# A gated-DeltaNet encoder layer: the products of k with k and q taken as split float32r products, half a batch at a time

## The chip, the cores and the metric

The kernel runs on one core of a Trainium2 chip. The metric is the device time of one execution in microseconds. An execution is one launch of the whole program: one encoder layer and the final norm, for a prompt of 1024 tokens and a sample of 256 tokens.

## The reference, cut to what matters

Each layer has a token-mixing block, a cross-attention into 256 memory tokens and a feed-forward block, for 1024 channels. The change lies in the token-mixing block's gated delta rule, which runs over 4 heads of 128 channels, forward and backward in time:

```
q = l2norm(heads(q, DN_DK)); k = l2norm(heads(k, DN_DK))
...
lower = where(strict, einsum('bhncd,bhnsd->bhncs', kb, k) * decay, 0.0)
tinv = triangular_solve(lower + eye, eye, ...)
u = einsum('bhncs,bhnsd->bhncd', tinv, v * beta[..., None])
a_intra = einsum('bhncd,bhnsd->bhncs', q, k) * decay
...
v_new = u_i - einsum('bhcd,bhde->bhce', w_i, state)
o = einsum('bhcd,bhde->bhce', qg_i, state) + einsum('bhcs,bhse->bhce', a_i, v_new)
state = state * exp(gl_i)[..., None, None] + einsum('bhcd,bhce->bhde', kg_i, v_new)
```

So every chunk of tokens needs two Gram matrices: the products of k with k, from which the triangular inverse comes, and the products of k with q, which weigh the chunk's own values.

## The kernel before, in words

**Numbers.** The large projections are float32 products split into float32r parts: an operand x becomes hi (x rounded by ScalarE's copy) and lo (x - hi), and a product is the sum of hi·hi, hi·lo and lo·hi (`mm3`, L110). The recurrence works with chunks of 128 tokens and with plain float32 products.

**Batches.** The 1280 tokens of 4 heads make 40 blocks of 128 x 128: each head's 1024 prompt tokens are one batch of 8 blocks (batches 0 to 3), the sample's 256 tokens of all four heads are the last (batch 4). `dn_batch` (L768) works through one batch: decays (L778 to L801), the products of k with k (L804 to L806), the inverse norms of k from their diagonals (L808 to L819, `rsqrt` at L230), the products of k with q and the matrices aT and X (L820 to L833), then X through DRAM into a layout in which VectorE solves 32 x 32 triangles (L837 to L865), back through DRAM into U and UT (L914 to L943), two levels of products that join the triangles (L946 to L984, whose first reads UT and X, "UT,gb" in the trace), and the scan over the blocks with its state (L988 to L1054).

**Names.** `dec` is the pair of decay tiles, one for each direction, in the tiles "gb0" and "gb1"; X is written over them in place (L832), so the trace says "gb". The tile `acc` is the convolved q, k or v, that is `q2`, `k2` and `v2`. `cw` holds the batch's columns of 8 numbers: ssk (the squared norms), r, r2, iv and bp.

**Order of work.** The program is written by a main generator (projections, tile by tile) and by side generators such as `dn_batch`. `mm` (L100) adds an estimate of each product to a clock; after each step of the main generator `pump` (L71) lets every side run whose time has come, and a side's `yield n` puts it off by n of that clock's nanoseconds. DEC is 1200. TensorE issues in the order in which this writes the program (L186). The order on the other engines is chosen at build time by the framework's scheduler, from when operands are ready in its own model of time. A matmul at the head of TensorE's queue that waits for somebody holds up all behind it, the main projections too.

**Banks.** PSUM is two pools of four banks of 512 float32 (L183, L184): `pm`, which the main projections use (one for each block of 512 or 256 tokens, until it is evacuated), and `pq` for small work. The products of k with k take two banks of `pm` for a batch, `pg` (L804); they hold them until X is made. The products of k with q take one bank of `pq` for each half (L823).

**Around it.** While the recurrence of one head runs, the main generator projects the next head's q, k and v (with their convolution, L696 to L752) and the gates (`gate_tile`), in plan order. The batches' scans overlap with the next batch's start: the decays and products of batch i + 1 are written when the inverse of batch i is done (`wait_for`, L776), beside batch i's scan. The tiles "UT0" and "UT1" (one buffer each) hold U's transposes until the inverse's end and the triangles (`XL`, L837) in between.

Of the kernel before, what the change touches and what calls it, by code (L numbers as in the profile page):

```python
# [9 lines left out]
F32R = mybir.dt.float32r  # L10
I32 = mybir.dt.int32
AF = mybir.ActivationFunctionType
ALU = mybir.AluOpType
# [4 lines left out]
P = 128  # L18
# [8 lines left out]
EPS = 1e-6  # L27
# [14 lines left out]
def f32(ap):  # L42
    return ap.bitcast(F32)


def quad(ps):
    return ps.rearrange("p (c t) -> p c t", t=P)
# [7 lines left out]
class Trunk:  # L55
# [44 lines left out]
    def mm(self, out, l, r, start=True, stop=True, more=False):  # L100
        n = 1
        for x in out.shape[1:]:
            n *= x
        if l.dtype == F32R:
            self.clock += max(n, 16) / 2.4 * (1 if n >= 256 else 4)
        else:
            self.clock += (4 * n / 2.4) if n > 1 else 2
        self.nc.tensor.matmul(out, l, r, start=start, stop=stop, skip_group_check=more)  # L108
# [59 lines left out]
def trunk_kernel(ctx: ExitStack, tc: tile.TileContext, a):  # L168
    nc = tc.nc
    V, S, G, T, SY = nc.vector, nc.scalar, nc.gpsimd, nc.tensor, nc.sync  # L170
    K = Trunk(ctx, tc, a)
    mm, mm3, tr, split = K.mm, K.mm3, K.tr, K.split
# [10 lines left out]
    pm = ctx.enter_context(pool("pm", 4, space=PSUM))  # L183
# [21 lines left out]
    two = lambda x: x.rearrange("h p (k n) -> p k h n", n=256)  # L205
# [11 lines left out]
    ident = cst[:, C_ID : C_ID + P]  # L217
# [6 lines left out]
    def bank(p=pq, tag="b"):  # L224
        return p.tile([P, 512], F32, tag=tag, name="bank")
# [4 lines left out]
    def rsqrt(y, x, scratch):  # L230
        V.tensor_scalar(out=y.bitcast(I32), in0=x.bitcast(I32), scalar1=-0.5, scalar2=float(0x5F3759DF), op0=ALU.mult, op1=ALU.add)
        for _ in range(3):
            V.scalar_tensor_tensor(out=scratch, in0=y, scalar=-0.5, in1=x, op0=ALU.mult, op1=ALU.mult)
            V.tensor_tensor(out=scratch, in0=scratch, in1=y, op=ALU.mult)
            end = V.scalar_tensor_tensor(out=y, in0=scratch, scalar=1.5, in1=y, op0=ALU.add, op1=ALU.mult).ins
        return end
# [176 lines left out]
    parts = []  # L413
# [9 lines left out]
    parts = [t[:, i * NS : (i + 1) * NS] for t in parts for i in range(2)]  # L423
# [3 lines left out]
    r = xp.tile([P, 512], F32, tag="nacc", name="seed", bufs=2)[:, :NS]  # L427
# [6 lines left out]
    hi, lo = x_h[2]  # L434
    rooms = [bank() for _ in range(3)]
    los = []
    for k in range(KT):
        if k in (5, 7):
            t = xp.tile([P, 512], F32, tag="nsq", name="nt", bufs=3)[:, :NS]
        else:  # L440
            at = min(k, 5)
            t = rooms[at % 3][:, at // 3 * NS : at // 3 * NS + NS]
# [3 lines left out]
        while los and (k == KT - 1 or los[0][0] < k):  # L446
            n, t = los.pop(0)
# [6 lines left out]
    pair = [(bank(), slice(512 * i, 512 * i + 512)) for i in range(2)]  # L454
# [32 lines left out]
    beta = cp.tile([P, 2, 40], F32, name="beta")  # L487
# [18 lines left out]
    s0, s1, var, rs, scr, mu = (sums[:, i, :] for i in range(6))  # L506
# [178 lines left out]
    qp = des.enter_context(pool("dn"))  # L685
# [73 lines left out]
    def big(tag, bufs=1):  # L759
        return qp.tile([P, 8, P], F32, tag=tag, name=tag, bufs=bufs)  # L760
# [3 lines left out]
    def wait_for(what, bi):  # L764
        while bi >= 0 and (what, bi) not in flags:
            yield 300

    def dn_batch(bi, qkv, chains):  # L768
        cs = slice(8 * bi, 8 * bi + 8)
# [3 lines left out]
        q2, k2 = qkv[:2]  # L773
        yield FIRST

        yield from wait_for("inverse", bi - 1)  # L776
        dec, bp, bpe, egl, eg, neg_eg = [], [], [], [], [], []
        for d in range(2):  # L778
            gb = big(f"gb{d}")
            SY.dma_start(gb, grd[d, cs, :].unsqueeze(0).to_broadcast([P, 8, P]))  # L780
            dec.append(gb)
        yield 2500
        for d in range(2):
            gb = dec[d]
# [16 lines left out]
            bp.append(bp_), bpe.append(bpe_), egl.append(egl_), eg.append(eg_), neg_eg.append(ne_)  # L801

        ssk, ssq, r, scr, r2, iv = (cw[:, i] for i in (0, 1, 2, 3, 6, 7))
        pg = [bank(pm), bank(pm)]  # L804
        for b in range(8):
            mm(pg[b // 4][:, (b % 4) * P : (b % 4 + 1) * P], k2[:, b, :], k2[:, b, :])  # L806
        junk = gs()[:, :P]
        for b in range(8):  # L808
            V.scalar_tensor_tensor(
                out=junk, in0=pg[b // 4][:, (b % 4) * P : (b % 4 + 1) * P], scalar=1.0, in1=ident, op0=ALU.mult, op1=ALU.mult,  # L810
                accum_out=ssk[:, b : b + 1])
            if b % 4 == 3:
                yield DEC
        V.tensor_scalar(out=scr, in0=ssk, scalar1=4.0 * EPS, scalar2=None, op0=ALU.add)
        rsqrt(r, scr, r2)
        V.tensor_tensor(out=r2, in0=r, in1=r, op=ALU.mult)
        V.scalar_tensor_tensor(out=iv, in0=r, scalar=0.5, in1=scr, op0=ALU.mult, op1=ALU.mult)
        for d in range(2):
            V.tensor_tensor(out=bp[d], in0=beta[:, d, cs], in1=r2, op=ALU.mult)  # L819
        aT = [big(f"aT{d}", 2) for d in range(2)]  # L820
        for hf in range(2):
            hs = slice(4 * hf, 4 * hf + 4)
            pa = bank()  # L823
            for c in range(4):
                mm(pa[:, c * P : (c + 1) * P], k2[:, 4 * hf + c, :], q2[:, 4 * hf + c, :])
            for d in range(2):
                V.tensor_tensor(out=aT[d][:, hs, :], in0=quad(pa), in1=dec[d][:, hs, :], op=ALU.mult)  # L827
            yield DEC
            for d in range(2):
                for c in range(4):  # L830
                    b = 4 * hf + c
                    V.scalar_tensor_tensor(out=dec[d][:, b, :], in0=pg[hf][:, c * P : (c + 1) * P], scalar=bp[d][:, b : b + 1], in1=dec[d][:, b, :], op0=ALU.mult, op1=ALU.mult)  # L832
                yield DEC  # L833
        X = dec

# [19 lines left out]
        for i in range(30, -1, -1):  # L855
            n, c = 32 - i, (i + 1) // 2
# [3 lines left out]
                out=t3, in0=u3[:, c:, i:],  # L860
                in1=XL[:, 32 * i + i : 32 * i + 32].unsqueeze(1).to_broadcast([P, m, n]), op=ALU.mult)
# [18 lines left out]
        for hf in range(2):  # L880
            hs = slice(4 * hf, 4 * hf + 4)
# [46 lines left out]
        for s in (0, 2):  # L928
            c = slice(16 * s, 16 * s + 16)
            SY.dma_start(own(UTm, s), vsd[bi][1, 0][:, c].rearrange("b c h j -> (c h) b j"))  # L930
            SY.dma_start(own(Um, s), vsd[bi][0, 1][:, c].rearrange("b c h j -> (c h) b j"))
        for s in range(4):
            c = slice(16 * s, 16 * s + 16)
# [14 lines left out]
        for level, mask in enumerate((m64, m128)):  # L948
# [7 lines left out]
            for hf, hs in enumerate(halves):  # L956
# [3 lines left out]
                for d in range(2):  # L960
                    V.scalar_tensor_tensor(
                        out=U[d][:, hs, :], in0=quad(pu), scalar=mine[:, 2 * level + d : 2 * level + d + 1], in1=U[d][:, hs, :],
                        op0=ALU.mult, op1=ALU.add)
# [34 lines left out]
        for step in range(nsteps):  # L998
            last = step == nsteps - 1
            for grp in groups:  # L1000
                ws, kg = {}, {}
                if not last:
                    for ch, (d, blks) in grp:
                        b = blks[step]
                        kg[ch] = sq128("sw", 6)
                        S.activation(kg[ch], ktm[:, b, :], AF.Copy, scale=bpe[d][:, b : b + 1])
                if step:
# [3 lines left out]
                    for i, (ch, (d, blks)) in enumerate(grp):  # L1011
                        b = blks[step]
# [4 lines left out]
                for i, (ch, (d, blks)) in enumerate(grp):  # L1017
                    b = blks[step]
                    mm(pc4(py, i), U[d][:, b, :], ws[ch] if step else vw[:, b, :])
                vt = {}  # L1020
                for i, (ch, (d, blks)) in enumerate(grp):
                    b = blks[step]
# [7 lines left out]
                if not last:  # L1030
# [3 lines left out]
                    for i, (ch, (d, blks)) in enumerate(grp):  # L1034
                        b = blks[step]
# [9 lines left out]
                for i, (ch, (d, blks)) in enumerate(grp):  # L1045
                    b = blks[step]
# [11 lines left out]
        for b in range(8):  # L1058
            junk = sq128("vt", 4)
# [398 lines left out]
    class OutProj:  # L1458
# [7 lines left out]
        def parts(self, m, b, ks, ps=None):  # L1466
            ps = bank(pm)[:, : BLOCKS[b][1]] if ps is None else ps
            if m == len(self.ws):
                self.ws.append(K.take())
            yield from proj(ps, self.ws[m], self.src, b, ks)  # L1470
            if (m, b) == (0, 0):
                K.ahead()
            self.first.append(ps)
# [224 lines left out]
    for h in range(HEADS):  # L1698
# [26 lines left out]
        if h == HEADS - 1:  # L1725
# [12 lines left out]
            for b in range(3):  # L1738
                hi, lo = o_h[b]
# [5 lines left out]
    op = OutProj(o_h, h3)  # L1745
# [116 lines left out]
    b12, r2 = ((Two(), Two()) for _ in range(2))  # L1862
# [557 lines left out]
DEC, CONV = 1200, 600  # L2420
# [85 lines left out]
```

## Time and profile before

| | before |
|---|---|
| runs (median of 3) | 2184.56 us (2183.62 to 2186.04) |
| profiled execution | 2183.43 us |
| its span in the profile | 2181.6 us |
| granted TensorE clock | 0.999 |
| VectorE / ScalarE / GpSimd busy | 1356.4 / 885.9 / 592.4 us |

The recurrence's five batches lie between about 150 and 830 us of the span. In the profile PE is TensorE's matmuls, PEld its weight loads, DVE VectorE, ACT ScalarE, POOL GpSimd, SP SyncE. Names of tiles are shown as output<-inputs, without buffer numbers. The timeline's rows are: start in us, duration in us, engine, line, operation, tiles, shape, count, and in brackets how long the engine sat idle before it and who ended that. Rows of one kind that follow each other are merged: their duration then runs from the first start to the last end. A float32 matmul stands in the trace as two passes, so "x16" is eight products.

### The profile page before, as it was taken

To read this page: it belongs to the slowest core of one execution; us is meant where nothing else is said; L and a number is where in the kernel's file an instruction comes from. 1 tells how busy PE (TensorE), PEld (TensorE's weight loads), DVE (VectorE), ACT (ScalarE), POOL (GpSimd) and SP (SyncE) were. 2 spreads that over 40 slices of the span, in tenths; PEclk is the share of its full clock that TensorE was granted. 3 is DMA by queue.
4 is the path that set the end of the run, shared out by engine and by line. 5 is a ranking of instruction groups with operands and counts; after the bars stand their busy time and mean duration, and the time that the engine had idled before them with its cause. 6 is when DMAs were issued, how large, how long until landed. Compare 5 with 4: busy or idle time off the path is not lost.

```text
span 2181.6 us, 31947 instructions
## 1 busy us (share of the span) xinstructions
PE 2168.0 (99%) x12184; PEld 1888.0 (87%) x12184; DVE 1356.4 (62%) x2615; ACT 885.9 (41%) x1651; POOL 592.4 (27%) x399
## 2 busy tenths in 40 slices
PE   9999999999999999999999999999999999999998
PEld 8988888888988888888988888888888888888888
DVE  7867688786874846677644556544434444478575
ACT  6533363544535553125544523332322323343454
POOL 2010100101001010052412432566666665200031
PEclk9999999999999999999999999999999999999999
DMA  5221323323244546631522421322222222493531
GB/s 195 92 93 57 109 63 96 82 66 95 75 122 121 171 133 228 204 128 58 175 73 111 156 97 64 104 87 83 83 78 81 83 97 91 149 347 119 205 112 59
DMA packets 194296, 253.04 MB, mean 116 GB/s; under 512 B 76932, under 2 KB 109268, under 8 KB 194142
## 3 DMA queue, kind: packets, MB, share of 16 engines
q1 hardware_dynamic: 177886, 227.14, 31.6%
q10 hardware_dynamic: 16256, 23.86, 3.0%
q8 instruction: 95, 1.56, 0.3%
q14 instruction: 59, 0.48, 0.1%
HBM read 178.02 MB, written 72.94 MB: 115 GB/s over the span
## 4 chain that ended last, share of the span: by engine, by line
PE 95%; DVE 2%; ACT 1%; DMA 1%; issue 0%; SPq 0%; POOL 0%; DVEq 0%; ACTq 0%; POOLq 0%
PE bank L108 94%; PE bank L121 1%; DMA braw<-gq 1%; DVE gb L832 0%; PE bank L398 0%; DVE aT L827 0%; DVE nt L298 0%; DVE nacc L260 0%; DMA uc<-usd 0%; DVE sw L1014 0%; POOL lo L126 0%; DVE wlo L126 0%; ACT junk L524 0%; ACT whi L125 0%; DVE bhl L126 0%
## 5 line engine op out<-in xcount | busy, mean ns | idle before, releaser
L108 PE MATMUL bank<-hi,whi 128*128 128x512 f32 (+1 forms) x1976 | 700.6, 355 | 0.0
L108 PE MATMUL bank<-lo,whi 128*128 128x512 f32 (+1 forms) x1976 | 687.0, 348 | 0.0
L108 PE MATMUL bank<-hi,wlo 128*128 128x512 f32 (+1 forms) x1976 | 686.6, 347 | 0.0
L108 PEld LDWEIGHTS bank<-hi,wlo 128*128 128x128 f32 x1976 | 373.6, 189 | 47.8
L108 PEld LDWEIGHTS bank<-hi,whi 128*128 128x128 f32 x1976 | 374.4, 189 | 45.1 <-issue 1.1
L108 PEld LDWEIGHTS bank<-lo,whi 128*128 128x128 f32 x1976 | 374.5, 190 | 43.3 <-issue 0.2
L126 POOL TENSOR_TENSOR wlo<-raw,whi 128x1024 fp32r<-128x1024 f32 x65 | 158.1, 2433 | 296.5 <-ACT whi L125 296.5
L125 ACT ACTIVATE whi<-raw 128x1024 fp32r<-128x1024 f32 (+1 forms) x136 | 137.0, 1009 | 249.1 <-PE bank L108 216.8
L126 DVE TENSOR_TENSOR wlo<-raw,whi 128x1024 fp32r<-128x1024 f32 (+1 forms) x71 | 80.8, 1141 | 74.7 <-ACT whi L125 74.4
L108 PE MATMUL bank<-bhl,whi 128*128 128x512 f32 x408 | 125.8, 390 | 0.0
L126 POOL TENSOR_TENSOR wlo<-x,whi 128x1024 fp32r<-128x1024 f32 x40 | 96.6, 2414 | 47.5 <-ACT whi L125 47.5
L2136 DVE TENSOR_TENSOR x<-x,bank 128x512 f32<-128x512 f32 x21 | 14.5, 689 | 124.4 <-ACT x L1931 124.4
L108 PEld LDWEIGHTS bank<-bhl,whi 128*128 128x128 f32 x408 | 76.5, 188 | 16.1
L710 DVE SCALAR_TENSOR_TENSOR acc<-craw,sm,acc 128x510 f32<-128x510 f32 (+1 forms) x96 | 73.2, 763 | 23.8 <-ACT acc L708 22.1
L1944 DVE SCALAR_TENSOR_TENSOR t<-t,x 128x512 f32<-128x512 f32 x42 | 63.9, 1521 | 28.7 <-ACT t L1943 28.7
L125 ACT ACTIVATE whi<-x 128x1024 fp32r<-128x1024 f32 (+1 forms) x48 | 49.2, 1025 | 77.5 <-PE bank L108 69.6
L108 PE MATMUL bank<-bhl,wlo 128*128 128x512 f32 x204 | 79.6, 390 | 0.2 <-DVE wlo L126 0.2
L1953 DVE SCALAR_TENSOR_TENSOR t<-bank,t 128x512 f32<-128x512 f32 (+1 forms) x44 | 24.5, 558 | 81.4 <-PE bank L108 81.4
L108 PE MATMUL bank<-bhl,ahl 128*128 128x512 f32 x312 | 75.0, 395 | 0.0
L1082 ACT ACTIVATE gs<-bank 128x512 f32<-128x512 f32 (+1 forms) x60 | 31.2, 520 | 101.2 <-PE bank L108 93.9
L1931 ACT ACTIVATE x<-bank 128x512 f32<-128x512 f32 x63 | 37.6, 597 | 82.0 <-PE bank L108 79.3
L108 PEld LDWEIGHTS bank<-bhl,ahl 128*128 128x128 f32 x312 | 58.7, 188 | 13.6
(420 smaller groups left out, 4462.6 us busy)
## 6 DMA issues: line engine op xcount, KB each, us to landing
raw<-in_w_gu SPq DMA_DIRECT2D x44, 512.0 KB, 3.3
braw<-gq SPq DMA_DIRECT2D x14, 1024.0 KB, 6.9
raw<-in_w_g SPq DMA_DIRECT2D x20, 512.0 KB, 3.3
gq<-t SPq DMA_DIRECT2D x33, 256.0 KB, 2.0
gtd<-gs ACTq DMA_DIRECT2D x32, 256.0 KB, 2.1
w<-in_w_dn SPq DMA_DIRECT2D x8, 1024.0 KB, 9.6
raw<-in_w_qkv SPq DMA_DIRECT2D x12, 512.0 KB, 3.4
gq<-r SPq DMA_DIRECT2D x22, 256.0 KB, 2.0
```

The costliest lines, as they stand in the source:

```text
L108: self.nc.tensor.matmul(out, l, r, start=start, stop=stop, skip_group_check=more)
L121: self.nc.tensor.transpose(out, x, ident)
L125: self.last_hi = self.nc.scalar.activation(hi, src, AF.Copy).ins
L126: (eng or self.nc.vector).tensor_tensor(out=lo, in0=src, in1=f32(hi), op=ALU.subtract)
L710: V.scalar_tensor_tensor(out=dst, in0=src, scalar=wj, in1=dst, op0=ALU.mult, op1=ALU.add)
L1082: S.activation(t, ps, AF.Tanh, scale=0.5)
L1931: S.activation(t, ps, AF.Copy)
L1944: V.scalar_tensor_tensor(out=t, in0=t, scalar=1.0, in1=src, op0=ALU.add, op1=ALU.mult)
L1953: V.scalar_tensor_tensor(out=out, in0=u, scalar=sign, in1=t, op0=ALU.mult, op1=ALU.mult)
L2136: V.tensor_tensor(out=c22, in0=c22, in1=pe, op=ALU.add)
```

## The change

The products of k with k and of k with q are made together, as split products in float32r. `parts(hf)` makes, for one half of a batch (4 blocks), kq_hi and kq_lo: ScalarE copies k2 and q2 to float32r side by side, GpSimd subtracts to get the rests. They live in the tiles "UT0" and "UT1". The first half's parts are written ahead of the decays, the second half's after the first half's products, into the same tiles. For each block three products of 256 columns (k's part against k's and q's parts side by side) go into one half of a `pm` bank; a half of the batch has two banks. The inverse norms, bp and X are then made for each half, and aT is read from the same banks, two blocks at a time. The second half's products stand four waits of DEC behind the first half's.

```diff
         yield from wait_for("inverse", bi - 1)
+        kq_hi, kq_lo = (qp.tile([P, 4, 2, P], F32R, tag=t, name="kq") for t in ("UT0", "UT1"))
+        def parts(hf):
+            hs = slice(4 * hf, 4 * hf + 4)
+            for i, t in enumerate((k2, q2)):
+                S.activation(kq_hi[:, :, i, :], t[:, hs, :], AF.Copy)
+                G.tensor_tensor(out=kq_lo[:, :, i, :], in0=t[:, hs, :], in1=f32(kq_hi[:, :, i, :]), op=ALU.subtract)
+
         dec, bp, bpe, egl, eg, neg_eg = [], [], [], [], [], []
...
+        parts(0)
         yield 2500
...
-        pg = [bank(pm), bank(pm)]
-        for b in range(8):
-            mm(pg[b // 4][:, (b % 4) * P : (b % 4 + 1) * P], k2[:, b, :], k2[:, b, :])
+        aT = [big(f"aT{d}", 2) for d in range(2)]
         junk = gs()[:, :P]
-        for b in range(8):
-            V.scalar_tensor_tensor(
-                out=junk, in0=pg[b // 4][:, (b % 4) * P : (b % 4 + 1) * P], scalar=1.0, in1=ident, op0=ALU.mult, op1=ALU.mult,
-                accum_out=ssk[:, b : b + 1])
-            if b % 4 == 3:
-                yield DEC
-        V.tensor_scalar(out=scr, in0=ssk, scalar1=4.0 * EPS, scalar2=None, op0=ALU.add)
-        rsqrt(r, scr, r2)
-        V.tensor_tensor(out=r2, in0=r, in1=r, op=ALU.mult)
-        V.scalar_tensor_tensor(out=iv, in0=r, scalar=0.5, in1=scr, op0=ALU.mult, op1=ALU.mult)
-        for d in range(2):
-            V.tensor_tensor(out=bp[d], in0=beta[:, d, cs], in1=r2, op=ALU.mult)
-        aT = [big(f"aT{d}", 2) for d in range(2)]
         for hf in range(2):
             hs = slice(4 * hf, 4 * hf + 4)
-            pa = bank()
+            pg = [bank(pm), bank(pm)]
+            pair = lambda c: pg[c // 2][:, (c % 2) * 256 : (c % 2) * 256 + 256]
             for c in range(4):
-                mm(pa[:, c * P : (c + 1) * P], k2[:, 4 * hf + c, :], q2[:, 4 * hf + c, :])
+                hi, lo = (t[:, c].rearrange("p i t -> p (i t)") for t in (kq_hi, kq_lo))
+                mm(pair(c), hi[:, :P], hi, True, False)
+                mm(pair(c), hi[:, :P], lo, False, False)
+                mm(pair(c), lo[:, :P], hi, False, True)
+            for c in range(4):
+                V.scalar_tensor_tensor(
+                    out=junk, in0=pair(c)[:, :P], scalar=1.0, in1=ident, op0=ALU.mult, op1=ALU.mult,
+                    accum_out=ssk[:, 4 * hf + c : 4 * hf + c + 1])
+            yield DEC
+            if hf == 0:
+                parts(1)
             for d in range(2):
-                V.tensor_tensor(out=aT[d][:, hs, :], in0=quad(pa), in1=dec[d][:, hs, :], op=ALU.mult)
+                for x in range(2):
+                    two = slice(4 * hf + 2 * x, 4 * hf + 2 * x + 2)
+                    V.tensor_tensor(out=aT[d][:, two, :], in0=pg[x].rearrange("p (c i t) -> p c i t", c=2, i=2)[:, :, 1, :], in1=dec[d][:, two, :], op=ALU.mult)
             yield DEC
+            V.tensor_scalar(out=scr[:, hs], in0=ssk[:, hs], scalar1=4.0 * EPS, scalar2=None, op0=ALU.add)
+            rsqrt(r[:, hs], scr[:, hs], r2[:, hs])
+            V.tensor_tensor(out=r2[:, hs], in0=r[:, hs], in1=r[:, hs], op=ALU.mult)
+            V.scalar_tensor_tensor(out=iv[:, hs], in0=r[:, hs], scalar=0.5, in1=scr[:, hs], op0=ALU.mult, op1=ALU.mult)
+            for d in range(2):
+                V.tensor_tensor(out=bp[d][:, hs], in0=beta[:, d, cs][:, hs], in1=r2[:, hs], op=ALU.mult)
             for d in range(2):
                 for c in range(4):
                     b = 4 * hf + c
-                    V.scalar_tensor_tensor(out=dec[d][:, b, :], in0=pg[hf][:, c * P : (c + 1) * P], scalar=bp[d][:, b : b + 1], in1=dec[d][:, b, :], op0=ALU.mult, op1=ALU.mult)
+                    V.scalar_tensor_tensor(out=dec[d][:, b, :], in0=pair(c)[:, :P], scalar=bp[d][:, b : b + 1], in1=dec[d][:, b, :], op0=ALU.mult, op1=ALU.mult)
                 yield DEC
         X = dec
```

## The prediction

> **What bounds the kernel now.** I read the page first (busy times, then the chain that ended last), then the groups of TensorE matmuls by shape, the waits, and the timeline of PE, DVE, ACT and POOL around the five batches of the recurrence.
>
> ```profile
> span 2181.6 us, 31947 instructions
> PE 2168.0 (99%) x12184; PEld 1888.0 (87%) x12184; DVE 1356.4 (62%) x2615; ACT 885.9 (41%) x1651; POOL 592.4 (27%) x399
> PE 95%; DVE 2%; ACT 1%; DMA 1%; issue 0%; SPq 0%; POOL 0%; DVEq 0%; ACTq 0%; POOLq 0%
> ```
>
> TensorE is busy 99% of the span and is 95% of the chain. It takes its instructions in the order in which the program wrote them. So only two things change the time: how long TensorE needs for its list, and how long the head of that list waits for somebody else. The change touches both, and I price them one after the other.
>
> **The products on TensorE.** The first batch, PE's timeline:
>
> ```profile
> 200.02 1.95 PE L108 MATMUL bank<-acc 128*128 128x128 f32 x16
> 201.73 0.48 PE L108 MATMUL bank<-hi,whi 128*128 128x512 f32 x1
> 202.04 0.40 PE L108 MATMUL bank<-lo,whi 128*128 128x512 f32 x1
> ...
> 203.18 0.28 PE L108 MATMUL bank<-hi,whi 128*128 128x256 f32 x1
> ...
> 204.62 1.05 PE L108 MATMUL bank<-acc 128*128 128x128 f32 x8
> 205.42 0.36 PE L108 MATMUL bank<-hi,whi 128*128 128x256 f32 x1
> 205.62 0.28 PE L108 MATMUL bank<-lo,whi 128*128 128x256 f32 x1
> ...
> 209.69 1.05 PE L108 MATMUL bank<-acc 128*128 128x128 f32 x8
> 210.50 0.48 PE L108 MATMUL bank<-hi,whi 128*128 128x512 f32 x1
> ```
>
> The second number is a pipelined duration; the price is the distance between starts. Each float32 product stands there as two passes. The eight k·k products take 201.73 - 200.02 = 1.71 us, the two blocks of four k·q products 0.80 and 0.81 us: 3.32 us a batch. After a block the first float32r matmul takes about 0.08 us longer (0.31 us from 201.73 to 202.04 where the rows of 512 columns stand 0.23 apart; 0.20 from 205.42 to 205.62 where 0.12 is usual). The new form is 24 float32r matmuls of 256 columns. The nearest row is the main work's own form: from 203.18 to 204.62 stand twelve of them, 0.12 us each, so 24 x 0.12 = 2.88 us a batch.
>
> In the first batch the three blocks stand between float32r matmuls, and three switches of 0.08 go too: 3.32 + 0.24 - 2.88 = 0.68 us saved. In the later batches the blocks follow float32 products of the scan, whose switch stays: 3.32 - 2.88 = 0.44 us. Sum: 0.68 + 4 x 0.44 = **2.4 us saved** of 2183. [...]
>
> **The wait in front of the second half.** Here is what can eat the saving. The pool pm has four PSUM banks, shared with the main projections. Before, a batch took two of them once. Now each half takes two, and the second half takes its pair while the first half's pair is still being read. One bank belongs to the main block in progress, two to the first half, so at most one is free: the third pair of the second half (its seventh matmul) has to wait until the first half's first bank has had its last reader, the second direction's L832. Behind it on PE everything queues: main projections and the scan of the previous batch.
>
> When does PE get there? From the end of the first half four waits of DEC have to pass.
>
> ```profile
> 329.07 1.95 PE L108 MATMUL bank<-acc 128*128 128x128 f32 x16
> ...
> 334.27 1.06 PE L108 MATMUL bank<-acc 128*128 128x128 f32 x8
> ...
> 340.88 1.06 PE L108 MATMUL bank<-acc 128*128 128x128 f32 x8
> ...
> 702.85 1.95 PE L108 MATMUL bank<-acc 128*128 128x128 f32 x16
> ...
> 707.84 1.06 PE L108 MATMUL bank<-acc 128*128 128x128 f32 x8
> ...
> 713.81 0.39 PE L108 MATMUL bank<-acc 128*128 128x128 f32 x2
> ```
>
> In the second batch two DEC lie between 329.07 and 334.27, less the block of 1.71: 1.75 each; three between 334.27 and 340.88, less 0.80: 1.94 each. Counted from the start of the first half, whose twelve matmuls take 1.44 us, the seventh matmul of the second comes six matmuls (0.72) after the four DEC: at 1.44 + 4 x 1.84 + 0.72 = 9.5 us. In the first batch (1.45 and 1.42 by the rows above) it is 7.9 us, in the last (1.64 and 1.72) 8.9 us.
>
> And when is the bank free? DVE in the second batch:
>
> ```profile
> 330.17 0.29 DVE L809 SCALAR_TENSOR_TENSOR gs<-bank,cst 128x128 f32<-128x128 f32 x1 [0.20 <-PE bank L108]
> ...
> 330.50 0.29 DVE L809 SCALAR_TENSOR_TENSOR gs<-bank,cst 128x128 f32<-128x128 f32 x1
> ...
> 332.33 0.60 DVE L1038 SCALAR_TENSOR_TENSOR st<-st,cw,bank 128x128 f32<-128x128 f32 x2
> ...
> 333.77 0.28 DVE L809 SCALAR_TENSOR_TENSOR gs<-bank,cst 128x128 f32<-128x128 f32 x1
> ...
> 335.21 0.16 DVE L814 TENSOR_SCALAR cw<-cw 128x8 f32<-128x8 f32 x1
> 335.37 0.69 DVE L827 TENSOR_TENSOR aT<-bank,gb 128x512 f32<-128x512 f32 x1
> 335.98 0.16 DVE L231 TENSOR_SCALAR cw<-cw 128x8 int32<-128x8 int32 x1
> ...
> 338.86 1.13 DVE L832 SCALAR_TENSOR_TENSOR gb<-bank,cw,gb 128x128 f32<-128x128 f32 x4
> 339.90 0.60 DVE L1038 SCALAR_TENSOR_TENSOR st<-st,cw,bank 128x128 f32<-128x128 f32 x2
> ...
> 341.33 1.12 DVE L832 SCALAR_TENSOR_TENSOR gb<-bank,cw,gb 128x128 f32<-128x128 f32 x4
> 342.36 0.60 DVE L1014 SCALAR_TENSOR_TENSOR sw<-bank,cw,vw 128x128 f32<-128x128 f32 x2
> ```
>
> The first L809 starts 1.1 us after its product's block; with six matmuls in a bank in place of eight passes I take 1.0. Then, per half: four L809 at 0.33 (330.17 to 330.50), 1.33; four aT products of 256 elements, 0.33 each as half of the 0.61 between 335.37 and 335.98 with some fixed part, 1.32; fifteen small instructions from L814 to L819, which take 338.86 - 335.21 less two aT (1.22), 2.43; L832 at 0.26 (four in 1.04 from 338.86), of which six stand ahead of the bank, 1.56. So 1.0 + 6.64 = 7.6 us with DVE to itself. It isn't: the scan's group from L1038 to L1053 takes 1.44 (332.33 to 333.77) and falls in once or twice, a pair of L1014 takes 0.5, an L715 0.3. That gives 9.9 us with one group and 11.3 with two, so PE waits 0.4 to 1.8 us, I take 1.2, in batches two to four. In the first batch no scan runs, but one gate evacuation does (L1084, below): 8.3 against 7.9, 0.4 us. In the last, one group and one pair: 9.5 against 8.9, 0.6 us. Sum 0.4 + 3.6 + 0.6 = 4.6 us.
>
> **The split itself.** ACT's copies and POOL's subtractions are new: four of each a batch, 128x512.
>
> ```profile
> 690.96 0.62 ACT L125 ACTIVATE mhi<-mraw 128x512 fp32r<-128x512 f32 x1
> ...
> L1084 DVE SCALAR_TENSOR_TENSOR gs<-gs,bank x12: 408/678/689, 197.0 to 253.3; 128x512 f32<-128x512 f32 x8, 128x256 f32<-128x256 f32 x4
> ...
> 740.04 1.28 POOL L901 TENSOR_TENSOR q2hl<-gs,q2hl 128x512 fp32r<-128x512 f32 x1
> ...
> 740.20 1.15 DVE L859 TENSOR_TENSOR W<-W,UT 128x3 f32<-128x3 f32 x1
> ...
> 742.13 0.15 DVE L859 TENSOR_TENSOR W<-W,UT 128x8 f32<-128x8 f32 x1
> ```
>
> The first half's parts need only k2 and q2, which are ready over 10 us ahead of the products: hidden. The second half's parts overwrite the first's tiles, so they start when its matmuls end, at 1.5 us: 0.62 + 2 x 1.28 and the handing over end at about 5 us; PE asks at 8.8 or, in the first batch, at 7.2: hidden, with 2 us of cover, and what exceeds the cover would stop PE one for one. ACT's copies stand ahead of the scan's copies on its queue for 0.62 us each; ACT is 41% busy and I cost that at nothing. But POOL then works while DVE does the small instructions, from 3.7 us on. The row at 740.20 shows what that does: a DVE product of two SBUF operands, 0.15 us by itself, took 1.15 and ended with POOL's subtraction. Thirteen of the fifteen small instructions read two SBUF operands. The cost is between 0 (POOL finished in time) and 2.6 us (both subtractions); I take 0.5 a batch, 2.5 us in all. PE's waits in front of the second half become 4.6 + 2.5 = **7.1 us**.
>
> **The chain behind it.** Both halves together now cost DVE 2 x (1.33 + 1.32 + 2.43 + 2.08) = 14.3 us where it was 8 x 0.33 + 2.43 + 4 x 0.61 + 16 x 0.26 = 11.7, so X, from which the inverse starts, is later by 2.6 + 0.5 = 3.1 us; PE's own list slides by the wait less the saving. How much room is there at the inverse's first product?
>
> ```profile
> 278.71 1.48 ACT L940 ACTIVATE UT<-uc 32x256 f32<-32x256 f32 x3
> 281.58 1.05 PE L108 MATMUL bank<-UT,gb 128*128 128x128 f32 x8
> ...
> 408.20 0.96 ACT L940 ACTIVATE UT<-uc 32x256 f32<-32x256 f32 x2
> 411.52 1.05 PE L108 MATMUL bank<-UT,gb 128*128 128x128 f32 x8
> ...
> 786.98 1.96 ACT L940 ACTIVATE UT<-uc 32x256 f32<-32x256 f32 x4
> 788.02 1.16 PE L108 MATMUL bank<-UT,gb 128*128 128x128 f32 x8
> ```
>
> 1.4 us in the first batch, 2.4 in the second, none in the last (PE starts while ACT still writes). First batch: 3.1 - (0.9 - 0.68) - 1.4 = 1.5 us of waiting. Batches two to four: 3.1 - (1.7 - 0.44) = 1.8, under 2.4: none. Last: 3.1 - (1.1 - 0.44) = 2.4. Sum **3.9 us**; from 0, if queues in between take it up, to 8.
>
> **Sum.** -2.4 + 7.1 + 3.9 = +8.6 us. The profiled execution took 2183.43 us (span 2181.6); it stands 1.13 under the median of 2184.56. So 2192.0 for it, **2193.2** as a median.
>
> **The rivals.**
> - *Only the products count.* DVE frees the bank in time and the chain finds room. For it: 7.6 us is all that DVE needs by itself, against 7.9 to 9.5. Against it: DVE has the scan's groups to serve. Price: -2.4 to +4.4 with part of the waits; bare, 2182.2. Chance 0.30.
> - *Faster.* DVE gets k·k and k·q of a half at once, so the first half of X no longer waits for the k·q block of 334.27, and the scan's products no longer queue behind sixteen passes. PE has small stalls in this stretch now: from 340.88 to 342.76 stand 1.88 us for 0.80 of products and three matmuls of 512 columns (0.31 + 2 x 0.23 by the rows of the first batch), 0.3 over. If every batch has one here and a like one at its inverse, and all go, 10 x 0.3 = 3.0 us; with the 2.4 saved, -5.4, 2179.2. It decides only if the first half's bank is free before 9.5 us in every batch. Chance 0.07.
> - *POOL and DVE exclude each other fully.* If each subtraction stops DVE for its whole 1.28 us, and each DVE product stops POOL, four of them take 5.1 us a batch, of which the second half's 2.6 stand in the path where I count 0.5. The waits grow by 5 x 2.1 = 10.5; the chain moves with PE. 2193.2 + 10.5 = 2203.7. Chance 0.15. [...]
>
> **How the numbers follow.** 0.2% of 2184.56, 4.4 us, is about what a measurement of this kernel can tell from no change. The forecast (waits and late chain, +4.4 to +14) has 0.48, POOL's lock 0.15, the products alone 0.30, faster 0.07. So slower 0.63, same 0.30, faster 0.07. The range runs from the products alone, 2182, to past the full lock, 2205.
>
> **What would show it.** In the profile after: 24 products a batch 0.12 us apart; a gap on PE in front of the seventh product of the second half, released by DVE's L832 (its new line), 0.4 to 2 us, five times; small DVE instructions of a microsecond beside POOL's subtractions; a longer gap in front of the inverse's first product in the first and last batch. I am wrong if the second half's products follow each other without a gap, or if the gap's releaser is POOL or ACT: then the split's own latency, which I called hidden, is the cost.

## The result and the profile after

| | before | after |
|---|---|---|
| runs (median) | 2184.56 us (2183.62 to 2186.04) | 2204.62 us (2203.91 to 2208.26, 5 runs) |
| profiled execution | 2183.43 us | 2205.66 us |
| its span | 2181.6 us | 2203.9 us |
| granted TensorE clock | 0.999 | 0.996 |
| VectorE / ScalarE / GpSimd busy | 1356.4 / 885.9 / 592.4 us | 1376.1 / 895.8 / 619.6 us |

The change makes the kernel slower: ratio 1.0096, 95% interval 1.0085 to 1.0107, 20.1 us by the medians. The forecast was 8.6 us, so the direction was right and the size was less than half of what came. The time lies inside the stated range, 2182 to 2205, but only just, and the upper end of that range stood for GpSimd and VectorE excluding each other fully, which the runs refuse below: that is luck. Lines of the kernel after are those of before plus 8 up to L808 and plus 12 from L837 on; the new ones are ScalarE's copy L781, GpSimd's subtraction L782, the diagonals L824, aT L833, the norms L835 to L840 and X, L844.

The page of the kernel after: first its span, busy times and then the chain that ended last, by engine and by line.

```profile
span 2203.9 us, 32031 instructions
PE 2173.2 (99%) x12144; PEld 1888.3 (86%) x12144; DVE 1376.1 (62%) x2710; ACT 895.8 (41%) x1671; POOL 619.6 (28%) x419
PE 89%; DVE 5%; DMA 2%; ACT 2%; issue 1%; SPq 1%; POOL 0%; DVEq 0%; ACTq 0%; POOLq 0%
```

TensorE's share of the chain fell from 95% to 89%: it now waits for others, for VectorE, DMAs and ScalarE. Busy time is modelled with pipelined ends, so I looked for the waits in TensorE's timeline. These are its rows at the new products and at the inverse's first product ("UT,gb"); the bracket is the idle time ahead of a row and who ended it.

```profile
206.34 0.39 PE L108 MATMUL bank<-hi,wlo 128*128 128x512 f32 x1
208.65 1.76 PE L108 MATMUL bank<-kq 128*128 128x256 f32 x12 [1.92 <-DVE gb L844]
210.21 0.63 PE L108 MATMUL bank<-hi,whi 128*128 128x512 f32 x1
...
472.69 1.71 PE L108 MATMUL bank<-kq 128*128 128x256 f32 x12
474.24 0.40 PE L108 MATMUL bank<-hi,whi 128*128 128x512 f32 x1
...
545.60 0.39 PE L108 MATMUL bank<-hi,wlo 128*128 128x512 f32 x1
548.74 2.07 PE L108 MATMUL bank<-UT,gb 128*128 128x128 f32 x8 [2.75 <-ACT UT L952]
550.46 0.77 PE L108 MATMUL bank<-hi,whi 128*128 128x512 f32 x1
551.04 0.63 PE L108 MATMUL bank<-lo,whi 128*128 128x512 f32 x1
...
680.37 0.40 PE L108 MATMUL bank<-hi,wlo 128*128 128x512 f32 x1
684.18 1.75 PE L108 MATMUL bank<-UT,gb 128*128 128x128 f32 x8 [3.41 <-DMA UT<-vsd]
...
726.34 0.96 PE L108 MATMUL bank<-kq 128*128 128x256 f32 x6
728.75 0.95 PE L108 MATMUL bank<-kq 128*128 128x256 f32 x6 [1.46 <-DVE gb L844]
...
808.78 1.16 PE L108 MATMUL bank<-UT,gb 128*128 128x128 f32 x8 [3.15 <-ACT UT L952]
```

Three things are to be seen.

*The products cost what was priced.* Twelve take 1.55 us from 472.69 to 474.24, with the switch of 0.07 us behind the scan's float32 products.

*The second half waits in two batches of five.* In batch 0 ahead of its first product, 208.65 - 206.34 less 0.23, 2.1 us; in batch 4 ahead of its seventh, 728.75 - 726.34 less 0.72 and 0.07 for the switch, 1.6 us. In batches 1 to 3 it doesn't wait (472.69).

*The larger waits stand at the inverse:* 2.9 us in batch 2 (548.74 - 545.60 less 0.23), 3.6 in batch 3, 3.3 in batch 4, and 1.05 in batch 0 (at 285.18, not shown).

Behind the waits of batches 0 and 2 the rows change: a matmul of 512 columns takes 0.43 us from start to start (551.04 to 551.46, the second start not shown; 0.23 is usual). The windows view shows why. Its columns after the stretch: length, busy time of PE, PEld, DVE, ACT and POOL, then the granted clock and the DMAs.

```profile
206.63:210.05 3.42, 1.50 (x13) 1.43 (x13) 3.13 (x15) 0.00 (x0) 0.00 (x0) 1.00 0.00 0
210.05:213.46 3.41, 3.41 (x11) 2.74 (x10) 3.34 (x14) 0.00 (x0) 0.95 (x1) 0.50 0.48 162
544.56:547.97 3.41, 1.43 (x7) 0.82 (x5) 3.34 (x5) 1.84 (x5) 0.10 (x1) 1.00 0.55 89
547.97:551.38 3.41, 2.64 (x10) 2.54 (x11) 2.20 (x5) 3.29 (x8) 0.13 (x2) 0.50 0.53 160
551.38:554.80 3.42, 3.42 (x13) 3.03 (x12) 1.66 (x3) 0.65 (x2) 0.00 (x0) 0.50 0.00 0
...
681.09:684.50 3.41, 0.32 (x3) 0.35 (x4) 0.00 (x0) 1.67 (x4) 0.00 (x0) 1.00 0.64 119
684.50:687.92 3.42, 3.42 (x16) 3.13 (x15) 0.69 (x1) 2.10 (x5) 0.00 (x0) 0.50 0.56 141
803.96:807.38 3.42, 1.67 (x8) 1.04 (x6) 0.00 (x0) 0.00 (x0) 0.95 (x1) 1.00 0.51 71
```

The windows are laid where the granted clock changes: the stretches at 0.50 begin and end on a grid of 3.413 us (from 210.05 to 547.97 it is 99 times, from there to 684.50 40 times). Each stretch follows a window in which TensorE was idle for 1.92, 1.98 or 3.09 us. The wait of 3.3 us in batch 4 fell into two windows, with 1.75 us idle (803.96) and 1.40 (the next, not shown), and no stretch followed it. The clock stood at half for four windows, 13.65 us, in which work of 6.8 us is lost. Before, no such stretch lies in the recurrence. The window before a stretch was not idle throughout: 1.92 us of 3.42 were enough in batch 0, 1.98 of 3.41 in batch 2.

The bill, by start-to-start distances on TensorE from 150 to 870 us less the usual 0.226, 0.12 and 0.11 us of a matmul of 512, 256 and 128 columns, after less before: waits at the inverse 12.3 - 1.2 = 11.1; in front of the second half 3.7; other and scan waits 2.8; gaps under 0.25 us 1.2; matmuls at half clock 6.1 (the rest of the 6.8 lies in the other terms); products -2.4, as priced. Together 22.5, against 22.3 between the spans. This closes the bill in size; why the waits arose is the matter of the experiments.

### The profile page after: what moved, and what is told of

Its sections match the earlier page's. It is cut to its first block, busy times and chain, and to the rows that moved or that the text cites. A ratio compares the mean times of both kernels' runs of the same rounds, so it can differ in the third digit from the quotient of the medians.

```text
span 2203.9 us, 32031 instructions
## 1 busy us (share of the span) xinstructions
PE 2173.2 (99%) x12144; PEld 1888.3 (86%) x12144; DVE 1376.1 (62%) x2710; ACT 895.8 (41%) x1671; POOL 619.6 (28%) x419
## 4 chain that ended last, share of the span: by engine, by line
PE 89%; DVE 5%; DMA 2%; ACT 2%; issue 1%; SPq 1%; POOL 0%; DVEq 0%; ACTq 0%; POOLq 0%
PE bank L108 88%; PE bank L121 1%; DVE acc L710 1%; DVE W L871 1%; DVE W L874 1%; DMA braw<-gq 1%; DVE wlo L126 0%; DVE U L973 0%; DVE lo L126 0%; DVE gb L803 0%; DMA W<-in_eye 0%; DMA vsd<-W 0%; DVE gs L710 0%; DMA stage<-ybd 0%; DMA xs<-in_xT 0%
```

## The experiments

The theory (L in the expectations): VectorE's doubled small work makes X late; the inverse's first product, whose place in TensorE's order is fixed, waits for it; and where the wait leaves a window idle for about 2 us, the clock halves. Its rivals: the banks, GpSimd, the new form of the products. The runs came in three groups, each with its own runs of the kernel before (2184.37, 2183.85 and 2183.46 us). The kernel after was measured beside 2184.56 us, so the kernel before itself reads up to 1.1 us apart, and differences from the kernel after are no finer than that. The order on VectorE and ScalarE is chosen anew for each version, so no edit changes one thing alone.

**VectorE's work alone, in the kernel before (dose).** Neither new products nor banks nor splits: only the inverse norms twice.

```diff
-        V.tensor_scalar(out=scr, in0=ssk, scalar1=4.0 * EPS, scalar2=None, op0=ALU.add)
-        rsqrt(r, scr, r2)
...
+        for again in range(2):
+            V.tensor_scalar(out=scr, in0=ssk, scalar1=4.0 * EPS, scalar2=None, op0=ALU.add)
+            rsqrt(r, scr, r2)
...
```

> The kernel before, with the fifteen small instructions of the inverse norms done twice over in each batch (same numbers, 3 us more of VectorE work ahead of X); products, banks and order as before. Theory L (VectorE's extra work makes X late, the inverse's first product then waits, and TensorE's clock is halved after a long wait): X ends 3 us later in every batch, gaps in front of the inverse's first product of 1 to 3 us in the first, third, fourth and last batch, 4 to 14 us slower than before. Rival B (the banks and the order in two halves are the cause): nothing of that is here, within 2 us of before.

Measured: 2190.22 us, ratio 1.0027 (1.0017 to 1.0036), 5.9 us more. No half-clock stretch (granted clock 0.999, as before). The time lies in L's range, at its low end, and the rival's "within 2 us" is out; but the waits stood elsewhere than L said. X ended 3.0 us later after the batch's first product in batch 0, but 1.2 in batches 1 to 3. At the inverse only batch 0 waited (1.05 us; all waits there 2.2 us, where the kernel before has 1.2). The scan waited 4.9 us, where it was 1.2. 3 us more of work a batch on an engine that is 62% busy cost 1.2 us a batch.

**The same, three times (dose3), and with room at the inverse (dose3_later).** The second moves the inverse's first product 1.5 us later in TensorE's order in two batches. The first edit is shown against dose, the second against dose3.

```diff
-        for again in range(2):
+        for again in range(3):
...
-        yield EXP / 2 + FIRST_EXP * (bi == 0)
+        yield EXP / 2 + FIRST_EXP * (bi == 0) + 1500 * (bi in (2, 3))
```

> The kernel before with the fifteen small instructions of the inverse norms done three times: about 6 us more of VectorE's work ahead of X, nothing else changed, and no new products, splits or banks. With one repetition (3 us) the inverse's first product waited 1.05 us in the first batch and 0.3 us in the next; a second repetition should add its 3 us to each of them in full. Late chain with the halved clock (L): waits of 3 to 4 us in front of the inverse in most batches, 13 to 16 us in all, some 5 us in the scan, and half-clock stretches behind two to four of the waits, of 3.4 us each (1.7 us lost by each): 2206 to 2214. Rival (the halved clock belongs to the new form of the products, to its switches or banks, and not to the waits): the same waits and no half-clock stretch, 2200 to 2206.

> The same, with the inverse's first product 1.5 us later in TensorE's order in batches 2 and 3. L: the waits there fall from about 3 to about 1.5 us, under the 2 us of idle time in a window that halved the clock elsewhere; no half-clock stretch behind these two, so the time falls by 3 us of waits plus what the clock lost there, 4.5 to 7 us under dose3's. Rival (room doesn't help, since VectorE's order moves with TensorE's, and the waits return in the scan): within 2 us of dose3's.

Measured: 2205.9 us, ratio 1.0103 (1.0086 to 1.0120), and 2204.86 us, ratio 1.0099 (1.0084 to 1.0114). So twice 3 us on VectorE in the kernel before cost 22.4 us, a little more than the whole change. At 2205.9 the time stands where the rival's range ends and L's begins and doesn't tell them apart; the clock does. It was halved without the new products, in three stretches (granted clock 0.996 in all), one of them here in the windows view of dose3:

```profile
618.57:621.99 3.42, 0.74 (x7) 0.53 (x5) 3.42 (x14) 0.00 (x0) 0.00 (x0) 1.00 0.54 163
621.99:625.40 3.41, 2.99 (x13) 2.90 (x14) 1.85 (x4) 1.07 (x3) 1.84 (x2) 0.50 0.45 67
```

The rival that puts the clock down to the new products falls. But the waits stood in another place than expected: only 1.9 us at the inverse (batch 0), and 3.3 us in each of batches 1 to 3, and 3.6 in batch 4, in the scan of the previous batch. VectorE's timeline of dose3 (L1015 is the scan's sw, L833 is X):

```profile
617.42 3.18 DVE L833 SCALAR_TENSOR_TENSOR gb<-bank,cw,gb 128x128 f32<-128x128 f32 x12
...
621.24 0.86 DVE L833 SCALAR_TENSOR_TENSOR gb<-bank,cw,gb 128x128 f32<-128x128 f32 x3
622.01 0.60 DVE L1015 SCALAR_TENSOR_TENSOR sw<-bank,cw,vw 128x128 f32<-128x128 f32 x2
```

and TensorE's:

```profile
619.03 0.28 PE L108 MATMUL bank<-hi,wlo 128*128 128x256 f32 x1
622.41 1.22 PE L108 MATMUL bank<-sw,U 128*128 128x128 f32 x4 [3.10 <-DVE sw L1015]
```

The scan's sw stands behind X on VectorE's queue, and TensorE waits for sw. So lateness on VectorE has two doors to TensorE, the inverse and the scan, and which one it takes depends on the order that the scheduler found. dose3_later is only 1.0 us under dose3, no more than the two runs' spread, where L had expected 4.5 to 7 and the rival within 2. It gave room at the inverse, where dose3 had no wait in these batches: batch 2's wait in the scan stayed at 3.3 us. The half-clock stretch of batch 3 went (the scan's wait there was 1.0 us; granted clock 1.00 from 560 to 700 us, where dose3 had 0.99) and one came in batch 4, where 3.4 us now stood at the inverse (0.99 from 700 to 830 us, where dose3 had 1.00).

**Less of VectorE's work in the kernel after (short_root).** One round of the root's iteration per half in place of three.

```diff
-        for _ in range(3):
+        for _ in range(rounds):
...
-            rsqrt(r[:, hs], scr[:, hs], r2[:, hs])
+            rsqrt(r[:, hs], scr[:, hs], r2[:, hs], 1)
```

> The changed kernel with one Newton round in place of three in each half's inverse norms (six small instructions fewer a half, 2.4 us of VectorE work fewer a batch; the norms are coarser). Theory L: X ends 2.4 us earlier, the gaps in front of the inverse's first product shrink from 11 us in all to under 4, the stretches at half clock in the third and fourth batch go: 2188 to 2195. Rival B: the banks are freed a little earlier, 2200 to 2205.

Measured: 2191.49 us, ratio 1.0035 (1.0022 to 1.0048), 13.1 us under the kernel after. No half-clock stretch (granted clock 0.999); the waits at the inverse fall from 12.3 to 1.2 us in all. TensorE's timeline in batch 2, to be compared with 548.74 above:

```profile
545.08 0.39 PE L108 MATMUL bank<-hi,wlo 128*128 128x512 f32 x1
545.31 1.05 PE L108 MATMUL bank<-UT,gb 128*128 128x128 f32 x8
```

Taking 2 x 6 small instructions of 0.2 us, 2.4 us of VectorE's work, out of each batch takes back 13.1 of the 20.1 us. What is left, 7.1 us over the kernel before, stands in the scan: waits of 10.5 us in all there, most of them for sw, which stands behind X as in dose3.

**More banks (banks).** The second half's products take their banks from the pool of the small work, so that they need not wait for the first half's.

```diff
-            pg = [bank(pm), bank(pm)]
+            pg = [bank(pm if hf == 0 else pq) for _ in range(2)]
```

> The changed kernel with the second half's two banks taken from the other pool (pq), so that it needn't wait for the first half's. Theory L: the gaps of 2.1 and 1.6 us in front of the second half go, with them the half clock of the first batch (1.7 us); the late chains of the other batches stay: 2196 to 2200. Rival B: all of it goes, 2183 to 2188. A third way: the scan of the batch before lacks banks in pq, and new gaps appear in front of its products: 2200 to 2215.

Measured: 2196.30 us, ratio 1.0053 (1.0036 to 1.0070). The time fits L's range, its reason only in part. The waits of batches 0 and 4 in front of the second half are gone, and so is every half-clock stretch (granted clock 0.999); but three waits of 0.9 us came in batches 1 to 3, inside the halves' products, for a bank of the other pool:

```profile
338.77 0.75 PE L108 MATMUL bank<-kq 128*128 128x256 f32 x5
340.32 0.86 PE L108 MATMUL bank<-kq 128*128 128x256 f32 x5 [0.80 <-DVE st L1050]
```

and the scan, which lives on that pool, waited 11.1 us in all where it had waited 1.9. The inverse waited 2.2 us in place of 12.3; L had said that the late chains stay, VectorE's work is the same as in the kernel after, and X was nearly as late (21.3 us after the first product in batches 2 and 3, where 21.6). So a late X is not enough for the waits at the inverse; what else it takes is read further below. New waits of the scan for banks were the third way of the expectation, and they came, but at a lower time than its 2200 to 2215.

**One inverse norm for the batch (one_root).** Banks as above, the norms once for all eight blocks, X block by block behind them. The second half's products stand three waits of DEC behind the first half's, in place of four.

```diff
-            rsqrt(r[:, hs], scr[:, hs], r2[:, hs])
...
+        rsqrt(r, scr, r2)
...
```

> Split products of both side by side, as in the changed kernel, but the second half's two banks come from pq and the inverse norms are made once for the batch, after both halves' products (15 small instructions a batch as before the change; X written block by block behind them). Theory L: VectorE has about the work of before, X ends no later than 1 us after that of before, no half clock; what is left are small gaps where the scan lacks banks of pq: 2182 to 2191. Rival P (the split products or their parts are slow in themselves): the loss stays, over 2196.

Measured: 2194.43 us, ratio 1.0048 (1.0033 to 1.0063), 3.4 us over L's range and 1.6 under the rival's. Inverse and clock went as expected (2.2 us of waits, no half-clock stretch, granted clock 0.999), though X was 2.2 to 2.3 us late in batches 1 to 3 where L had said 1 at most; the scan cost 12.6 us, mostly waits of 0.86 and of 1.3 to 1.5 us in each of batches 1 to 4, for a bank that VectorE was still to read (L1053, and X at the last one in batch 4):

```profile
338.55 0.60 PE L108 MATMUL bank<-vt,sw 128*128 128x128 f32 x4
339.85 0.71 PE L108 MATMUL bank<-vt,aT 128*128 128x128 f32 x4 [0.70 <-DVE st L1053]
```

**Without GpSimd (no_pool).** The subtractions are left out, and the rounded parts stand in for the rests in the products.

```diff
-                G.tensor_tensor(out=kq_lo[:, :, i, :], in0=t[:, hs, :], in1=f32(kq_hi[:, :, i, :]), op=ALU.subtract)
...
-                hi, lo = (t[:, c].rearrange("p i t -> p (i t)") for t in (kq_hi, kq_lo))
+                hi, lo = (t[:, c].rearrange("p i t -> p (i t)") for t in (kq_hi, kq_hi))
```

> The changed kernel without GpSimd's subtractions: the rests are left out and the rounded parts stand in their place in the products (as many products, the numbers are wrong by that). Theory L: the subtractions stop VectorE only where a small instruction meets one, which is in the first and the last batch (0.5 to 1.2 us each): 2198 to 2204. [...]

Measured: 2200.82 us, ratio 1.0078 (1.0063 to 1.0093), 3.8 us under the kernel after; the two intervals overlap. The time is in L's range. The waits in front of the second half fall from 2.1 and 1.6 to 1.5 and 1.0 us, those at the inverse stay (11.5 us in all), and three half-clock stretches of 3.4 us stay (granted clock 0.99 from 430 to 560, from 560 to 700 and from 700 to 830 us). GpSimd is a part of the bank waits, 1.1 us, and not the main cause.

**Filling the waits (fill).** Products of zeros, 28 passes of 0.43 us in all, ahead of the inverse's first product in batches 2 to 4 and ahead of the second half in batch 0. They read nothing that is late and change no result.

```diff
+            if bi == 0 and hf == 1:
+                hold(2, bank())
...
+                if bi > 1 and level == 0 and hf == 0:
+                    hold(4, pz)
```

> The changed kernel with idle products put where TensorE waits: four products of zeros with 512 columns (3.4 us) ahead of the inverse's first product in batches 2, 3 and 4, two (1.7 us) ahead of the second half in batch 0. They do no work. If the half clock behind a wait is a cause of its own (theory L), the stretches at half clock go while the waits are only filled: 5 to 7 us faster than the changed kernel, 2197 to 2200. If the clock follows something else, no gain: 2204 to 2208.

Measured: 2201.72 us, ratio 1.0078 (1.0063 to 1.0093), 2.9 us under the kernel after. The two intervals overlap, and the time lies between the two ranges expected, so the clock decides: the half-clock stretches are all gone (granted clock 0.999). The waits are no shorter (below) and only filled, so it is the idle time in them that halves the clock. TensorE's timeline in batch 3:

```profile
677.83 3.18 PE L398 MATMUL bank<-shared 128*128 128x512 f32 x7
682.02 1.13 PE L108 MATMUL bank<-UT,gb 128*128 128x128 f32 x8 [1.01 <-DMA UT<-vsd]
```

The gain is less than the 5 to 7 us expected: the fillers, 28 x 0.43 = 12.0 us, and the waits of 1.4 and 0.55 us left behind them make 14.0, where the four waits had been 2.1 + 2.9 + 3.6 + 3.3 = 11.9. So 2.1 of the clock's 6.8 us went to fillers that were too long; that makes -4.7, where the spans differ by 3.4 and the medians by 2.9. The rest I can't place.

**Room at the inverse (later23).** The kernel after with the inverse's first product 1.5 us later in TensorE's order in batches 2 and 3.

```diff
-        yield EXP / 2 + FIRST_EXP * (bi == 0)
+        yield EXP / 2 + FIRST_EXP * (bi == 0) + 1500 * (bi in (2, 3))
```

> The changed kernel with the inverse's first product written 1.5 us later in TensorE's order in batches 2 and 3 (more main products ahead of it), all else as it was. Theory L: the gaps there, 2.9 and 3.6 us, get 1.5 us shorter each, and at 1.4 and 2.1 us the half clock behind them (6.8 less 1.7 us of loss) goes at least in batch 2: 2196 to 2200. Rival: the chain goes with TensorE's order, the gap moves along and stays as long: 2203 to 2206.

Measured: 2196.34 us, ratio 1.0058 (1.0042 to 1.0075), 8.3 us under the kernel after, with the computation unchanged. Batch 3's wait is gone, batch 2's is

```profile
549.07 1.16 PE L108 MATMUL bank<-UT,gb 128*128 128x128 f32 x8 [0.71 <-ACT UT L952]
```

and the only half-clock stretch left is batch 0's (granted clock 0.998 in all). The time is in L's range, and the rival, that the wait moves along, is out. But the waits fell by more than the 1.5 us of room: 2.0 us in batch 2, 3.6 in batch 3, and batch 4's 3.3, where nothing was edited. In the recurrence the inverse's waits fell by 9.7 us and the matmuls' loss at half clock by 4.6, and 3.8 us of waits came back in the scan: 10.5 us, of which 1.4 were lost elsewhere in the program (the spans differ by 9.1).

None of these versions is as fast as the kernel before. By the prediction's sum there was little to win: the products' 2.4 us is all that the change takes off TensorE's list.

## Why the prediction was right in its sign and wrong in its size

*The products, -2.4 us: right.* 1.44 to 1.51 us for twelve, without the switch, where 1.44 was priced.

*The wait in front of the second half, 7.1 us with 2.5 for GpSimd's subtractions: 3.7 measured, these included, and in other batches than priced.* It should have been 1.2 us in each of batches 1 to 3, and the subtractions' part besides; it was nothing there, which the prediction had named as a sign of being wrong. VectorE's timeline, batch 2 of the kernel after:

```profile
471.67 2.16 DVE L844 SCALAR_TENSOR_TENSOR gb<-bank,cw,gb 128x128 f32<-128x128 f32 x8
```

The sixth of these ends at 471.67 + 6 x 0.26 = 473.2; the products began at 463.3, so the bank was free after 9.9 us, the lower of the two times worked out (one group of the scan). TensorE asked at 472.69 + 6 x 0.12 = 473.4, 10.1 us, not 9.5. The bank was priced at 10.7 us (9.5 and a wait of 1.2): two sizes, off by 0.8 and 0.6 us, cancelled the wait. In batch 0 it was 2.1 where 0.4 was priced: ahead of the first product, so no bank at all was free. In batch 4, ahead of the seventh, it was 1.6 where 0.6 was priced. I had counted one bank for the main work, and in batch 0 the gates' block still held one until its evacuation (L1096), which stood behind X on VectorE.

*GpSimd's subtractions beside VectorE, 2.5 us: about 1.1.* VectorE's rows beside the subtractions, batches 0 and 4:

```profile
203.74 0.70 DVE L835 TENSOR_SCALAR cw<-cw 128x4 f32<-128x4 f32 x1
...
720.86 0.50 DVE L835 TENSOR_SCALAR cw<-cw 128x4 f32<-128x4 f32 x1
721.39 1.22 DVE L231 TENSOR_SCALAR cw<-cw 128x4 int32<-128x4 int32 x1
722.65 0.16 DVE L233 SCALAR_TENSOR_TENSOR cw<-cw 128x4 f32<-128x4 f32 x1
```

and GpSimd's:

```profile
201.85 2.57 POOL L782 TENSOR_TENSOR kq<-acc,kq 128x512 fp32r<-128x512 f32 x2 [4.47 <-ACT kq L781]
...
720.04 2.55 POOL L782 TENSOR_TENSOR kq<-acc,kq 128x512 fp32r<-128x512 f32 x2 [11.90 <-ACT kq L781]
```

The two subtractions of 1.28 us are merged into one row. One instruction of batch 0 is held until the second of them ends (0.70 us where 0.16 is usual), and in batch 4 one is held by each (0.50 and 1.22), as the row at 740.20 had shown. VectorE lost 0.5 and 1.4 us by it; by no_pool the waits on TensorE are 1.1 us shorter without it. In batches 1 to 3 GpSimd was done 0.7 to 0.8 us before the small instructions began. That the two exclude each other fully, the third rival, falls, though its 2203.7 us is near the measured time: without any subtraction the kernel still takes 2200.82 us, so that nearness is chance. That the split's own latency is hidden held: no row has GpSimd or ScalarE as the releaser of these products.

*The chain behind it, 3.9 us: the step that failed.* The waits at the inverse measured 11.1 us over the kernel before. The step is "Batches two to four: 3.1 - (1.7 - 0.44) = 1.8, under 2.4: none." (counted from one, so batches 1 to 3 here): it gave nothing to batches 2 and 3, which waited 2.9 and 3.6 us. X was 2.6 us later in these batches, counted from the batch's first product (21.6 us where 19.0), so the 2.6 in the sum's 3.1 was good; the other 0.5 was for GpSimd's subtractions, which cost nothing here. The error was to carry 2.6 us through the rest of the chain unchanged. VectorE's and then ScalarE's rows of the kernel after, batch 2, behind X:

```profile
498.18 1.23 DVE L126 TENSOR_TENSOR wlo<-raw,whi 128x1024 fp32r<-128x1024 f32 x1 [3.90 <-ACT whi L125]
499.43 1.13 DVE L862 COPY UT<-W 64x1024 f32<-64x1024 f32 x1
...
507.01 0.16 DVE L871 TENSOR_TENSOR W<-W,UT 128x2 f32<-128x2 f32 x1 [6.26 <-ACT W L866]
```

```profile
499.75 1.03 ACTq L1087 DMA_DIRECT2D yod<-gs  x2
505.89 1.09 ACT L866 ACTIVATE W<-W 128x512 f32<-128x512 f32 x1 [5.59 <-DMA W<-in_eye]
```

The copy L862 stood behind a weight split on VectorE, and VectorE sat idle 3.9 us for that split's input; the load that follows the copy landed beside the previous batch's stores; ScalarE's L866 began 6.5 us after the copy, where before it was 3.9 (its rows there, VectorE's and ScalarE's):

```profile
488.99 1.12 DVE L850 COPY UT<-W 64x1024 f32<-64x1024 f32 x1
```

```profile
492.91 1.10 ACT L854 ACTIVATE W<-W 128x512 f32<-128x512 f32 x1 [0.86 <-DMA W<-in_eye]
```

So the triangles' solve started 8.4 us late (43.7 us after the batch's first product, 35.3 before), and the inverse's operands were ready 6.3 us late, against a room of 2.3. In batch 1, where X was as late, the solve started 3.9 us late and TensorE did not wait: the growth is no law, it depends on what a late step meets. The run banks shows this for batches 2 and 3 too. There X was nearly as late (21.3 us), but the copy did not stand behind a weight split and its load went ahead of the stores. VectorE's, ScalarE's and TensorE's rows of banks, batch 2:

```profile
496.14 1.12 DVE L862 COPY UT<-W 64x1024 f32<-64x1024 f32 x1
```

```profile
500.11 1.13 ACT L866 ACTIVATE W<-W 128x512 f32<-128x512 f32 x1
...
502.71 0.91 ACTq L1087 DMA_DIRECT2D yod<-gs  x2
```

```profile
546.80 1.05 PE L108 MATMUL bank<-UT,gb 128*128 128x128 f32 x8
```

L866 began 4.0 us after the copy, the solve started 3.2 us late, and TensorE did not wait at the inverse. So these queues, and not X's 2.6 us alone, made the waits of batches 2 and 3. How much is the weight split's and how much the stores' stays open, since no run has one without the other.

In batches 0 and 4 the sum was off elsewhere. X itself was 6.4 and 8.2 us late there (20.5 us after the first product where 14.1, and 25.0 where 16.8), not 3.1. The waits, 1.05 us where 1.5 was priced and 3.3 where 2.4, came near because TensorE's own list had slid too, by some 3 us ahead of either wait where 0.2 and 0.7 were priced.

*The halved clock, 6.8 us: not in the sum at all.* Each of the four windows at half clock cost 1.7 us more, half of its 3.41. The prediction counted each microsecond of waiting once.

*Two small terms, 1.1 us each, were missing too:* waits at 543.52 for GpSimd's q2hl and at 769.95 in the main products.

The rivals: the products alone and faster had 0.37 of the chance between them, and both assumed that a VectorE that is 62% busy takes up its extra work somewhere. The dose in the kernel before shows that it doesn't: 3 us a batch gave 5.9 us, 6 us a batch 22.4.

## What to carry to other kernels

- Where a short chain of one engine ends in another engine's fixed order, its slack is what the nearest waiter has, not its idle share. Measure that slack by a dose: do the suspected work twice and look at the time, before the change is made.
- A late step doesn't stay equally late. Look what it would be queued behind if it came 3 us later, on each engine and DMA that it passes. The same 2.6 us cost nothing in one batch here and 3.6 us in another.
- Waits on TensorE that leave a window idle for about 2 us were dearer than their length here: 1.92, 1.98 and 3.09 us of idle time were followed by windows at half clock, with 1.7 us lost in each. A wait of 3.3 us that fell into two windows, with 1.75 and 1.40 us, was not.

## What the runs showed of the hardware

The halved clock was the surprise. In the kernel after, between 150 and 830 us, each of the three windows with 1.92 us or more of TensorE's idle time was followed by a stretch at half clock, as was dose3's at 618.57 with 2.68, and none of the three with 1.40 to 1.75 us (the ends of matmuls are modelled, so no exact bound follows). Of these stretches of the kernel after two last one window, 3.41 us, and one two, 6.83: that one has 0.77 us of idle time in its first window at half clock (547.97), the other two have none. The other was the small instructions of 0.50 to 1.22 us beside GpSimd's subtractions: their operands are one SBUF tile and constants, not two tiles, which I had taken to be the condition; what the condition is, no run shows.
